# The end of a two-layer decoder kernel: a gate moved into the weights, a shorter final norm, stores on two queues

## The chip, the cores and the metric

The kernel runs on one core of a Trainium2 chip. A core has engines that run side by side, each with its own list of instructions: TensorE (matmul), VectorE (elementwise work), ScalarE (activation functions, copies and casts), GpSimd and SyncE, whose queue issues most of the transfers. An engine waits at an instruction until what it needs has been signalled by the others. The metric is the device time of one execution in microseconds; lower is better.

## The reference, cut to what matters

The reference is a decoder trunk of two layers over 512 rows of 1024 columns in fp32. Only its end counts here: the MLP of the second layer, its gated residual, and the final norm over the columns of each row.

```python
for layer in range(DEPTH):
    ...
    shift, scale, gate = ada_modulation(c, ada_w[layer, 1], ada_b[layer, 1])
    h = rms_norm(x, norm_w[layer, 1]) * (1.0 + scale) + shift
    x = x + (gate * squared_relu_mlp(h, mlp_w1[layer], mlp_w2[layer])).astype(x.dtype)
return rms_norm(x, final_norm_w)

def rms_norm(x, w):
    y = xf * lax.rsqrt(jnp.mean(xf * xf, axis=-1, keepdims=True) + EPS)
    return (y * w.astype(jnp.float32)).astype(x.dtype)
```

`gate` has one value for each of the 1024 columns, so gate * (g @ w2) is the same as g @ (w2 with its columns scaled by the gate).

## The kernel before, in words

Each fp32 operand of a matmul is split into a high part (`wh`, `gh`; a cast by ScalarE) and a low part (`wl`, `gl`; raw minus high, by VectorE), and each product takes three matmuls: high by high, low by high, high by low. The second layer's down projection runs over eight groups of 512 inner features. Six of them are done as pairs in a scheme that combines quarter products. The last two groups (`gs[0]` and `gs[1]`, r = 0 and 1) go through `Pair.direct`, the last stage of the kernel.

In `direct` the output is cut into two column halves (q = 0, 1; 512 columns each) and four row blocks of 128 rows (`hf`, `i`; tb = 2 hf + i). For each q and each row block, 24 matmuls of 128x512 fill one bank: r = 0, 1, then f = 0 to 3, then the three of each product. The banks are named sc, sc, tp, po in turn, again for q = 1. The weights are split ahead by `split`, four tiles of 128x512 each: keys 11 and 21 for q = 0 (made earlier), key 12 (r = 0) and key 22 (r = 1) for q = 1. Key 12 is split at the start of `direct`, key 22 within the fourth q = 0 block, after its matmuls are written and before its evacuation.

The other work: `gate_b[q]` is the gate spread over all rows (by TensorE, then copied from the bank by ScalarE); `fwb[q]` is the final norm's weight, loaded into all rows; `xT` is the residual, loaded from a scratch tensor. In the trace and in the order lists all of these are tiles called `end`: in the lists end_8978 and end_8979 are `gate_b[0]` and `gate_b[1]`, end_8980 and end_8981 are `fwb[0]` and `fwb[1]`, end_8970 to end_8977 are `xT`. The partial sums of the earlier pairs are the tiles x_132 to x_137 and two `acc`; at the start of `direct` 16 VectorE operations multiply each by the gate and add the residual. The raw weights are w_1413 to w_1416 (key 12) and w_1417 to w_1420 (key 22).

After a block VectorE multiplies the bank by the gate and adds it to the sum tile; ScalarE squares the sum with a row total into a column of `ss` (`square`). With q = 1 `finish` makes the row factor: small VectorE and ScalarE operations on one column, among them a logarithm and an exponential for the inverse square root, and one refining step. Then VectorE scales both halves by the row factor and by `fwb`, and SyncE's queue stores each.

The order: from this stage on VectorE and TensorE keep the order in which the program is written (`V` and `TE` are `_InOrder`; every one of their instructions shows as line 81, that of the helper). The lists of ScalarE and of the queue are set by the scheduler.

Of the kernel before, what the change touches and what calls it, by code (L numbers as in the profile page):

```python
# [15 lines left out]
ALU = mybir.AluOpType  # L16
AX = mybir.AxisListType

P = 128
T = 512  # L20
D = 1024
# [5 lines left out]
EPS = 1e-6  # L27
# [57 lines left out]
def trunk(ctx: ExitStack, tc: tile.TileContext, ins, out):  # L85
    nc = tc.nc
    V, S, G, TE = nc.vector, nc.scalar, nc.gpsimd, nc.tensor
# [6 lines left out]
    wsplit = ctx.enter_context(tc.tile_pool(name="wsplit", bufs=4))  # L94
# [9 lines left out]
    def nm(s):  # L104
        uid[0] += 1
        return f"{s}_{uid[0]}"
# [4 lines left out]
    def sc_ps():  # L111
        return ps_sc.tile([P, 512], F32, tag="sc", name=nm("sc"))
# [27 lines left out]
    rows = fpool.tile([P, 2 * P], F32, name="rows")  # L140
# [44 lines left out]
    def square(j, hf, n_, fast=False):  # L185


        xj, sums = x[j][:, HALVES[hf]], sqsum.get(hf)
        if n_ == 0:
            sums = sqsum[hf] = [wk("sqsum", (P, HALF))]  # L190
        elif n_ == 1 and fast:
            sums.append(pp.tile([P, HALF], F32, tag="sqsum2", name=nm("sqsum2")))
        i = n_ % len(sums)
        if n_ == 0 or n_ == 1 and fast:
            S.activation(sums[i], xj, AF.Square)
            return lambda: None
        sq = wk("acc", (P, T))[:, 0:HALF] if fast else wk("sq", (P, HALF))
        S.activation(sq, xj, AF.Square)

        def add():  # L200
            e = V if i == 1 or n_ == ND - 1 else G
            e.tensor_tensor(sums[i], sums[i], sq, op=ALU.add)
            if n_ == ND - 1 and fast:
                V.tensor_tensor(sums[0], sums[0], sums[1], op=ALU.add)

        return add
# [125 lines left out]
    def load(dst, src):  # L332

        if isinstance(V, _InOrder):
            anchor[0] = Q.dma_start(dst, src)
        else:
            with tc.issue_after(anchor[0].ins):
                nc.sync.dma_start(dst, src)
# [183 lines left out]
    class Seam(Steps):  # L522
# [18 lines left out]
        def square(self, kind, hf, j):  # L541
            n_ = self.counts[kind, hf] = self.counts.get((kind, hf), -1) + 1
            self.adds[hf, j] = square(j, hf, n_, kind == "y")
# [51 lines left out]
    def bank4():  # L595
        four[0] += 1
        return (sc_ps, sc_ps, tp_ps, po_ps)[(four[0] - 1) % 4]()
# [7 lines left out]
    V, S, G, TE = [_InOrder(tc, e) for e in (V, S, G, TE)]  # L605
# [740 lines left out]
    V, S, G, TE = nc.vector, nc.scalar, nc.gpsimd, nc.tensor  # L1346
# [187 lines left out]
    V, S, G, TE = [_InOrder(tc, e) for e in (V, S, G, TE)]  # L1534
# [13 lines left out]
    V, S, G, TE = nc.vector, nc.scalar, nc.gpsimd, nc.tensor  # L1548
# [6 lines left out]
    wsplit2 = spare.pop()  # L1555
    fp = ctx.enter_context(tc.tile_pool(name="fin", bufs=1))
    ss = fp.tile([P, 16], F32, name="ss")
# [3 lines left out]
    for tb in range(NT):  # L1561
        rt = wraw.tile([P, RAW], F32, tag="raw", name=nm("xT"))
        for q in range(2):
            ps = sc_ps()
# [8 lines left out]
    sums = {(k, i): free[2 * k - 2 + i] for k in range(1, 8) for i in range(2)}  # L1573
    C11, C12, C21, C22 = 2, 3, 4, 5

    def each(*all_):

        all_ = [a[0] if isinstance(a, list) and len(a) == 1 else a for a in all_]
        if not any(isinstance(a, list) for a in all_):
            return [all_]  # L1580
        return [[a[i] if isinstance(a, list) else a[:, i * HALF : (i + 1) * HALF] for a in all_] for i in range(2)]
# [3 lines left out]
    class Pair:  # L1585
# [9 lines left out]
                        load(t, mlp1.w2[:, 4 * (2 * n + r) + f, q * T : (q + 1) * T])  # L1595
                        self.raw[f"{r + 1}{q + 1}", f] = t

        def split(self, key, pool=wsplit):

            w = []  # L1600
            for f in range(4):
                if f % 2 == 0:
                    th = pool.tile([P, RAW], F32R, tag="wh", name=nm("wh"))
                    tl = pool.tile([P, RAW], F32R, tag="wl", name=nm("wl"))
                cs = slice(f % 2 * T, (f % 2 + 1) * T)
                S.copy(th[:, cs], self.raw[key, f])  # L1606
                V.tensor_tensor(tl[:, cs], self.raw[key, f], th[:, cs].bitcast(F32), op=ALU.subtract)  # L1607
                w.append((th[:, cs], tl[:, cs]))
            return w
# [87 lines left out]


        def direct(self, weights):
            later = [self.split("12", wsplit2)]  # L1700
            for q in range(2):
                for tb in range(NT):
                    for t, g_, x_ in each(sums[2 + tb // 2 * 2 + q, tb % 2], gate_b[q], xT[tb, q]):
                        V.tensor_tensor(t, t, g_, op=ALU.mult)
                        V.tensor_tensor(t, t, x_, op=ALU.add)
            for q in range(2):
                w = later if q else weights
                for hf in range(2):
                    for i in range(2):
                        k = 2 + 2 * hf + q  # L1710
                        ps = bank4()
                        ts = slice((2 * hf + i) * P, (2 * hf + i + 1) * P)
                        for r in range(2):
                            gh, gl = self.gs[r]
                            for f in range(4):
                                wh, wl = w[r][f]
                                TE.matmul(ps, gh[:, f, ts], wh, start=r + f == 0, stop=False)
                                TE.matmul(ps, gh[:, f, ts], wl, start=False, stop=False)
                                TE.matmul(ps, gl[:, f, ts], wh, start=False, stop=r == 1 and f == 3)
                        if k == 4 and i == 1:  # L1720
                            later.append(self.split("22"))
                        (t,) = sums[k, i]
                        V.tensor_tensor(ps, ps, gate_b[q], op=ALU.mult)
                        V.tensor_tensor(t, t, ps, op=ALU.add)
                        self.square(k, hf, q, i)
                        if q:
                            self.finish(k - 1, k, hf, i)

        def square(self, k, hf, q, i):
            (t,) = sums[k, i]  # L1730
            tb = 2 * hf + i
            S.activation(junk, t, AF.Square, accum_out=ss[:, 2 * tb + q : 2 * tb + q + 1])

        def finish(self, k0, k1, hf, i):
            tb = 2 * hf + i
            r, y = ss[:, 8 + tb : 9 + tb], ss[:, 12 + tb : 13 + tb]
            V.tensor_tensor(r, ss[:, 2 * tb : 2 * tb + 1], ss[:, 2 * tb + 1 : 2 * tb + 2], op=ALU.add)
            V.tensor_scalar(r, r, 1.0 / D, EPS, op0=ALU.mult, op1=ALU.add)
            S.activation(y, r, AF.Ln)
            S.activation(y, y, AF.Exp, scale=-0.5)  # L1740
            V.scalar_tensor_tensor(r, r, y, y, op0=ALU.mult, op1=ALU.mult)
            V.tensor_scalar(r, r, -0.5, 1.5, op0=ALU.mult, op1=ALU.add)
            V.tensor_tensor(r, r, y, op=ALU.mult)
            for q, k in enumerate((k0, k1)):
                (t,) = sums[k, i]
                V.scalar_tensor_tensor(t, t, r, fwb[q], op0=ALU.mult, op1=ALU.mult)
                nc.sync.dma_start(out[0, tb * P : (tb + 1) * P, q * T : (q + 1) * T], t)

    def merge():

# [35 lines left out]
    V, weights = _InOrder(tc, nc.vector), []  # L1786
# [8 lines left out]
    gate_b, fwb = [late_tile(8 + q) for q in range(2)], [late_tile(10 + q) for q in range(2)]  # L1795
    junk = late_tile(12)
    for q in range(2):
        load(fwb[q], ins["final_norm_w"][q * T : (q + 1) * T].partition_broadcast(P))
        ps = (tp_ps, po_ps)[q]()
        for j in range(4):  # L1800
            TE.matmul(ps[:, j * P : (j + 1) * P],
                      mlp1.gate[:, 4 * q + j : 4 * q + j + 1].broadcast_to([P, P]), ident, start=True, stop=True)
        S.copy(gate_b[q], ps)
        for tb in range(NT):
            load(xT[tb, q], xT_dram[tb][:, q * T : (q + 1) * T])
# [24 lines left out]
```

## Time and profile before

| | |
|---|---|
| time, median of 3 runs | 1001.47 us (998.39 to 1001.85) |
| profiled execution, own time | 997.38 us |
| its span, first to last instruction | 995.7 us |
| granted TensorE clock, mean | 0.995 |
| TensorE busy | 968.0 us, 97% |
| VectorE busy | 675.7 us, 68% |
| ScalarE busy | 490.2 us, 49% |
| GpSimd busy | 188.0 us, 19% |

The shares are means over the whole span; the stage of the change is its last 50 us. Whether an operation there counts is read from who waits for whom: an engine that waits for nothing but TensorE has time to spare, and TensorE's next block is late only if its weights or its bank are late.

### The profile page before, as it was taken

Reading aid. Unit: us, or ns where it says so; the run is one execution under the profiler, and the core shown is the slowest. Engines: PE = TensorE matmul, PEld = TensorE weight load, DVE = VectorE, ACT = ScalarE, POOL = GpSimd, SP = SyncE. Lnnn points to the kernel's source line nnn. Section 1 sums busy time; section 2 is a strip of 40 time slices with the busy share of each in tenths; the row PEclk is TensorE's granted clock in tenths of the full one; section 3 lists DMA queues with packets and bytes.
Section 4 is the critical chain, followed back from the end, with each engine's and each line's share of the span. In section 5 each row is a group of like instructions: output and inputs, shape, how many; then the busy total and the mean of one; then the engine's idle time right before and its main releaser. Section 6 shows DMA issues by size and latency. Waiting matters only on the chain.

```text
span 995.7 us, 14343 instructions
## 1 busy us (share of the span) xinstructions
PE 968.0 (97%) x5392; PEld 804.6 (81%) x5392; DVE 675.7 (68%) x1181; ACT 490.2 (49%) x913; POOL 188.0 (19%) x136
## 2 busy tenths in 40 slices
PE   6989999998999999999999999999999999999996
PEld 5568888788987778787777899998788788778885
DVE  3678886666886757666665427859557856886385
ACT  6566657665542433333343435665664544455511
POOL 0033436456120201111122345400000000000000
PEclk9999999999999999999999999999999999999999
DMA  9973566442375656465566312172451253042202
GB/s 309 339 173 106 170 188 217 154 141 64 107 240 183 221 157 214 134 208 187 170 211 207 107 49 83 60 245 78 127 169 43 85 161 93 0 152 102 74 34 84
DMA packets 119367, 145.57 MB, mean 146 GB/s; under 512 B 5782, under 2 KB 86018, under 8 KB 119298
## 3 DMA queue, kind: packets, MB, share of 16 engines
q1 hardware_dynamic: 119138, 144.59, 46.9%
q8 instruction: 42, 0.69, 0.3%
q14 instruction: 27, 0.22, 0.1%
q10 hardware_dynamic: 160, 0.07, 0.0%
HBM read 140.25 MB, written 4.39 MB: 145 GB/s over the span
## 4 chain that ended last, share of the span: by engine, by line
PE 87%; DVE 5%; issue 2%; DMA 2%; POOL 2%; ACT 1%; SPq 1%; DVEq 0%; POOLq 0%; ACTq 0%
PE mm L81 33%; PE mm L370 10%; PE sc L81 10%; PE mm L372 10%; PE mm L371 10%; PE po L81 5%; PE tp L81 5%; PE ad L81 2%; DMA adaw<-in_ada_w 1%; SPq L81 1%; DVE wl L1607 1%; POOL wl L81 1%; PE ad L283 1%; POOL sqsum L81 1%; DMA xin<-in_x 1%
## 5 line engine op out<-in xcount | busy, mean ns | idle before, releaser
L364 ACT CAST wh<-w 128x1024 fp32r<-128x1024 f32 x82 | 85.8, 1050 | 110.0 <-PE mm L371 80.2
L81 PE MATMUL mm<-hh,wl 128*128 128x512 f32 (+1 forms) x312 | 116.1, 379 | 2.0 <-DVE wl L366 2.0
L366 DVE TENSOR_TENSOR wl<-w,wh 128x1024 fp32r<-128x1024 f32 x76 | 100.0, 1320 | 24.3 <-ACT wh L364 23.2
L81 PE MATMUL mm<-hh,wh 128*128 128x512 f32 (+1 forms) x312 | 116.3, 380 | 0.0
L81 PE MATMUL mm<-hl,wh 128*128 128x512 f32 (+1 forms) x312 | 115.5, 377 | 0.0
L81 POOL TENSOR_TENSOR wl<-w,wh 128x1024 fp32r<-128x1024 f32 x36 | 87.6, 2444 | 79.9 <-ACT wh L81 77.1
L371 PE MATMUL mm<-hl,wh 128*128 128x512 f32 (+1 forms) x256 | 95.7, 376 | 0.0
L372 PE MATMUL mm<-hh,wl 128*128 128x512 f32 (+1 forms) x256 | 95.5, 375 | 0.0
L370 PE MATMUL mm<-hh,wh 128*128 128x512 f32 (+1 forms) x256 | 94.3, 377 | 0.0
L1606 ACT CAST wh<-w 128x512 fp32r<-128x512 f32 x100 | 56.9, 619 | 53.2 <-PE po L81 21.9
L370 PE MATMUL mm<-gh,wh 128*128 128x512 f32 x192 | 75.9, 395 | 0.0
L371 PE MATMUL mm<-gl,wh 128*128 128x512 f32 x192 | 74.8, 390 | 0.0
L372 PE MATMUL mm<-gh,wl 128*128 128x512 f32 x192 | 74.8, 390 | 0.0
L81 PEld LDWEIGHTS mm<-hh,wl 128*128 128x128 f32 x312 | 58.7, 188 | 15.6 <-DVE wl L366 4.0
L81 PEld LDWEIGHTS mm<-hh,wh 128*128 128x128 f32 x312 | 58.9, 189 | 11.6 <-ACT wh L364 0.6
L81 PEld LDWEIGHTS mm<-hl,wh 128*128 128x128 f32 x312 | 58.9, 189 | 11.3
L1607 DVE TENSOR_TENSOR wl<-w,wh 128x512 fp32r<-128x512 f32 x84 | 54.7, 689 | 17.7 <-ACT wh L1606 17.5
L248 DVE SCALAR_TENSOR_TENSOR acc<-adaw,sc,acc 128x512 f32<-128x512 f32 x60 | 46.7, 778 | 21.0 <-DMA adaw<-in_ada_w 20.4
L274 POOL TENSOR_TENSOR adaw<-adaw 128x512 f32<-128x512 f32 x12 | 15.7, 1306 | 232.4 <-ACT adaw L272 199.4
L375 DVE SCALAR_TENSOR_TENSOR x<-mm,mod,x 128x512 f32<-128x512 f32 x48 | 35.7, 746 | 31.8 <-PE mm L372 31.8
L81 ACT CAST wh<-w 128x1024 fp32r<-128x1024 f32 (+1 forms) x44 | 43.8, 1004 | 25.8 <-DMA w<-in_attn_w_in 9.3
L372 PEld LDWEIGHTS mm<-hh,wl 128*128 128x128 f32 x256 | 48.2, 188 | 9.6 <-issue 0.8
(499 smaller groups left out, 2488.9 us busy)
## 6 DMA issues: line engine op xcount, KB each, us to landing
w<-in_mlp_w SPq DMA_DIRECT2D x98, 512.0 KB, 4.1
adaw<-in_ada_w SPq DMA_DIRECT2D x92, 512.0 KB, 4.6
w<-in_mlp_w SPq DMA_DIRECT2D x64, 256.0 KB, 3.7
w<-in_attn_w_in SPq DMA_DIRECT2D x8, 512.0 KB, 3.6
w<-in_attn_w_out SPq DMA_DIRECT2D x8, 512.0 KB, 3.5
w<-in_attn_w_in SPq DMA_DIRECT2D x8, 392.0 KB, 7.9
xin<-in_x SPq DMA_DIRECT2D x4, 512.0 KB, 5.7
adaw<-in_ada_w SPq DMA_DIRECT2D x8, 256.0 KB, 6.1
```

Source lines behind the costliest of these rows:

```text
L81: return lambda *args, **kw: self.tc.keep_in_program_order(f(*args, **kw))
L248: V.scalar_tensor_tensor(acc, rv, sk, acc, op0=ALU.mult, op1=ALU.add)
L274: G.tensor_tensor(rv[:, 0], rv[:, 0], rv[:, 1], op=ALU.add)
L283: TE.matmul(ps[32 * j : 32 * j + 32], one_col[:, 31 - r : 63 - r], self.acc[:, j * P : (j + 1) * P], start=True, stop=True)
L364: S.copy(th[:, :n], rt[:, :n])
L366: return w, lambda e: e.tensor_tensor(tl[:, :n], rt[:, :n], th[:, :n].bitcast(F32), op=ALU.subtract)
L370: TE.matmul(ps, wh, ah, start=start, stop=False)
L371: TE.matmul(ps, wh, al, start=False, stop=False)
L372: TE.matmul(ps, wl, ah, start=False, stop=stop)
L375: V.scalar_tensor_tensor(x[j][:, ts], ps, g, x[j][:, ts], op0=ALU.mult, op1=ALU.add)
L1606: S.copy(th[:, cs], self.raw[key, f])
L1607: V.tensor_tensor(tl[:, cs], self.raw[key, f], th[:, cs].bitcast(F32), op=ALU.subtract)
```

## The change

- `split` takes a `scale`: for keys 12 and 22 each raw weight tile is multiplied by `gate_b[1]` in place, by VectorE, before its cast. The gate multiply of the bank stays for q = 0 only.
- With q = 0 `square` now also scales the row total (divide by 1024, add EPS) and multiplies the sum tile by `fwb[0]`.
- `finish` has one small operation ahead of the logarithm instead of two and two behind the exponential instead of three; the factor -0.5 of the refining step goes into `fwb`, which is scaled by it after its load.
- The first column half is multiplied by the row factor on ScalarE and stored from ScalarE's queue; the second stays on VectorE and SyncE's queue.

```diff
-        def split(self, key, pool=wsplit):
+        def split(self, key, pool=wsplit, scale=None):
 
             w = []
             for f in range(4):
+                if scale is not None:
+                    V.tensor_tensor(self.raw[key, f], self.raw[key, f], scale, op=ALU.mult)
                 if f % 2 == 0:
                     th = pool.tile([P, RAW], F32R, tag="wh", name=nm("wh"))
...
         def direct(self, weights):
-            later = [self.split("12", wsplit2)]
+            later = [self.split("12", wsplit2, gate_b[1])]
...
                         if k == 4 and i == 1:
-                            later.append(self.split("22"))
+                            later.append(self.split("22", scale=gate_b[1]))
                         (t,) = sums[k, i]
-                        V.tensor_tensor(ps, ps, gate_b[q], op=ALU.mult)
+                        if q == 0:
+                            V.tensor_tensor(ps, ps, gate_b[q], op=ALU.mult)
                         V.tensor_tensor(t, t, ps, op=ALU.add)
                         self.square(k, hf, q, i)
...
             S.activation(junk, t, AF.Square, accum_out=ss[:, 2 * tb + q : 2 * tb + q + 1])
+            if q == 0:
+                r = ss[:, 8 + tb : 9 + tb]
+                V.tensor_scalar(r, ss[:, 2 * tb : 2 * tb + 1], 1.0 / D, EPS, op0=ALU.mult, op1=ALU.add)
+                V.tensor_tensor(t, t, fwb[q], op=ALU.mult)
 
         def finish(self, k0, k1, hf, i):
             tb = 2 * hf + i
             r, y = ss[:, 8 + tb : 9 + tb], ss[:, 12 + tb : 13 + tb]
-            V.tensor_tensor(r, ss[:, 2 * tb : 2 * tb + 1], ss[:, 2 * tb + 1 : 2 * tb + 2], op=ALU.add)
-            V.tensor_scalar(r, r, 1.0 / D, EPS, op0=ALU.mult, op1=ALU.add)
+            V.scalar_tensor_tensor(r, ss[:, 2 * tb + 1 : 2 * tb + 2], 1.0 / D, r, op0=ALU.mult, op1=ALU.add)
             S.activation(y, r, AF.Ln)
             S.activation(y, y, AF.Exp, scale=-0.5)
             V.scalar_tensor_tensor(r, r, y, y, op0=ALU.mult, op1=ALU.mult)
-            V.tensor_scalar(r, r, -0.5, 1.5, op0=ALU.mult, op1=ALU.add)
-            V.tensor_tensor(r, r, y, op=ALU.mult)
-            for q, k in enumerate((k0, k1)):
-                (t,) = sums[k, i]
-                V.scalar_tensor_tensor(t, t, r, fwb[q], op0=ALU.mult, op1=ALU.mult)
-                nc.sync.dma_start(out[0, tb * P : (tb + 1) * P, q * T : (q + 1) * T], t)
+            V.scalar_tensor_tensor(r, r, 3.0, y, op0=ALU.subtract, op1=ALU.mult)
+            rows = out[0, tb * P : (tb + 1) * P, :]
+            (t0,), (t1,) = sums[k0, i], sums[k1, i]
+            S.mul(t0, t0, r)
+            V.scalar_tensor_tensor(t1, t1, r, fwb[1], op0=ALU.mult, op1=ALU.mult)
+            nc.scalar.dma_start(rows[:, 0:T], t0)
+            nc.sync.dma_start(rows[:, T:D], t1)
...
         load(fwb[q], ins["final_norm_w"][q * T : (q + 1) * T].partition_broadcast(P))
+        V.tensor_scalar(fwb[q], fwb[q], -0.5, None, op0=ALU.mult)
```

TensorE's list is the same row for row, and GpSimd's too. The lists of VectorE and ScalarE differ only from the last up-projection block on.

VectorE at the start of `direct`, before: the last `gl`, the split of key 12, the partial sums.

```order
L81 TENSOR_TENSOR gl_8769<-r_8965,gh_8768 128x512
L81 TENSOR_TENSOR wl_9006<-w_1413_8786,wh_9005 128x512
L81 TENSOR_TENSOR wl_9006<-w_1414_8788,wh_9005 128x512
L81 TENSOR_TENSOR wl_9012<-w_1415_8790,wh_9011 128x512
L81 TENSOR_TENSOR wl_9012<-w_1416_8792,wh_9011 128x512
L81 TENSOR_TENSOR x_132<-x_132,end_8978 128x512
```

The same place after the change.

```order
L81 TENSOR_TENSOR gl_8769<-r_8965,gh_8768 128x512
L81 TENSOR_SCALAR end_8980<-end_8980 128x512
L81 TENSOR_SCALAR end_8981<-end_8981 128x512
L81 TENSOR_TENSOR w_1413_8786<-w_1413_8786,end_8979 128x512
L81 TENSOR_TENSOR wl_9009<-w_1413_8786,wh_9008 128x512
L81 TENSOR_TENSOR w_1414_8788<-w_1414_8788,end_8979 128x512
L81 TENSOR_TENSOR wl_9009<-w_1414_8788,wh_9008 128x512
```

The two scalings of `fwb` now stand ahead of the split, and a gate multiply stands ahead of each subtraction; w_1415 and w_1416 follow in the same way.

VectorE at the end of the q = 0 blocks, before: the third evacuation (bank tp), the split of key 22, the fourth evacuation (bank po).

```order
L81 TENSOR_TENSOR tp_9089<-tp_9089,end_8978 128x512
L81 TENSOR_TENSOR x_136<-x_136,tp_9089 128x512
L81 TENSOR_TENSOR wl_9143<-w_1417_8794,wh_9142 128x512
L81 TENSOR_TENSOR wl_9143<-w_1418_8796,wh_9142 128x512
L81 TENSOR_TENSOR wl_9149<-w_1419_8798,wh_9148 128x512
L81 TENSOR_TENSOR wl_9149<-w_1420_8800,wh_9148 128x512
L81 TENSOR_TENSOR po_9117<-po_9117,end_8978 128x512
```

The same place after the change.

```order
L81 TENSOR_TENSOR tp_9099<-tp_9099,end_8978 128x512
L81 TENSOR_TENSOR x_136<-x_136,tp_9099 128x512
L81 TENSOR_SCALAR ss<-ss 128x1
L81 TENSOR_TENSOR x_136<-x_136,end_8980 128x512
L81 TENSOR_TENSOR w_1417_8794<-w_1417_8794,end_8979 128x512
L81 TENSOR_TENSOR wl_9156<-w_1417_8794,wh_9155 128x512
L81 TENSOR_TENSOR w_1418_8796<-w_1418_8796,end_8979 128x512
L81 TENSOR_TENSOR wl_9156<-w_1418_8796,wh_9155 128x512
```

A small operation on `ss`, which reads ScalarE's row total, and the multiply by `fwb[0]` now stand behind each q = 0 evacuation, so also ahead of the split; the split has a multiply ahead of each subtraction, and w_1419 and w_1420 follow in the same way.

VectorE's last rows, the fourth q = 1 block, before.

```order
L81 TENSOR_TENSOR po_9274<-po_9274,end_8979 128x512
L81 TENSOR_TENSOR acc_6834<-acc_6834,po_9274 128x512
L81 TENSOR_TENSOR ss<-ss 128x1
L81 TENSOR_SCALAR ss<-ss 128x1
L81 SCALAR_TENSOR_TENSOR ss<-ss 128x1
L81 TENSOR_SCALAR ss<-ss 128x1
L81 TENSOR_TENSOR ss<-ss 128x1
L81 SCALAR_TENSOR_TENSOR x_137<-x_137,ss,end_8980 128x512
L81 SCALAR_TENSOR_TENSOR acc_6834<-acc_6834,ss,end_8981 128x512
```

ScalarE's last rows after the change; VectorE keeps for this block the add, three small operations and the scaling of acc_6834.

```order
L1735 ACTIVATE end_8982,ss<-acc_6834 128x512
L1745 ACTIVATE ss<-ss 128x1
L1746 ACTIVATE ss<-ss 128x1
L1751 ACTIVATE x_137<-x_137,ss 128x512
L1753 DMA out<-x_137 128x512
```

The scaling of x_137 and its store have moved from VectorE and SyncE's queue to ScalarE and its queue.

## Rows read from the trace of the kernel before

**Rows 1.** Page, part 4: shares of the chain that ended last.

```profile
PE 87%; DVE 5%; issue 2%; DMA 2%; POOL 2%; ACT 1%; SPq 1%; DVEq 0%; POOLq 0%; ACTq 0%
```

**Rows 2.** Chain in order of time from 944 us: start, length, what.

```profile
943.83 10.93 PE sc L81 x48
...
965.64 10.88 PE sc L81 x48
...
987.44 0.71 DVE po L81
```

**Rows 3.** Timeline of VectorE, 938 to 970: start, length, operation, [idle before, releaser].

```profile
945.53 0.69 DVE L81 TENSOR_TENSOR gl<-r,gh 128x512 fp32r<-128x512 f32 x1 [6.40 <-ACT r L417]
946.14 2.49 DVE L81 TENSOR_TENSOR wl<-w,wh 128x512 fp32r<-128x512 f32 x4
948.54 8.06 DVE L81 TENSOR_TENSOR x<-x,end 128x512 f32<-128x512 f32 x12
...
959.18 0.69 DVE L81 TENSOR_TENSOR sc<-sc,end 128x512 f32<-128x512 f32 x1
...
963.17 2.49 DVE L81 TENSOR_TENSOR wl<-w,wh 128x512 fp32r<-128x512 f32 x4
```

**Rows 4.** Timeline of SyncE's queue and of ScalarE near 942.

```profile
941.75 0.42 SPq L81 DMA_DIRECT2D end<-in_final_norm_w  x1
...
941.85 1.14 ACT L1606 CAST wh<-w 128x512 fp32r<-128x512 f32 x2 [1.66 <-PE mm L81]
```

**Rows 5.** DMA issues from 941.5 to 942.1: size, us from issue to landing.

```profile
end<-in_final_norm_w SPq DMA_DIRECT2D x1, 256.0 KB, 5.1
```

**Rows 6.** Timeline from the last add to the last store's issue.

```profile
988.17 0.69 DVE L81 TENSOR_TENSOR acc<-acc,po 128x512 f32<-128x512 f32 x1
988.89 0.63 ACT L1732 ACTIVATE end<-acc 128x512 f32<-128x512 f32 x1 [3.86 <-DVE acc L81]
...
989.65 0.16 DVE L81 TENSOR_TENSOR ss<-ss 128x1 f32<-128x1 f32 x1 [0.79 <-ACT end L1732]
...
990.03 0.20 ACT L1739 ACTIVATE ss<-ss 128x1 f32<-128x1 f32 x1 [0.41 <-DVE ss L81]
...
990.50 0.22 DVE L81 SCALAR_TENSOR_TENSOR ss<-ss 128x1 f32<-128x1 f32 x1 [0.51 <-ACT ss L1740]
...
991.14 0.75 DVE L81 SCALAR_TENSOR_TENSOR x<-x,ss,end 128x512 f32<-128x512 f32 x1
...
991.92 0.33 SPq L1747 DMA_DIRECT2D out<-x  x1
992.58 0.33 SPq L1747 DMA_DIRECT2D out<-acc  x1
```

**Rows 7.** Groups by line and form: count, busy us, mean ns, idle before.

```profile
L1606 ACT CAST wh<-w 128x512 fp32r<-128x512 f32 x100 | 56.9, 619 | 53.2 <-PE po L81 21.9 <-PE mm L81 21.1 <-PE sc L81 9.7
...
L272 ACT ACTIVATE adaw<-adaw,sc 128x512 f32<-128x512 f32 x24 | 16.1, 716 | 41.0 <-DMA adaw<-in_ada_w 37.9 <-DVE wl L366 3.1
...
L81 DVE TENSOR_TENSOR x<-x,end 128x512 f32<-128x512 f32 x12 | 7.8, 689 | 0.2
...
L81 DVE TENSOR_SCALAR acc<-adaw,sc 128x512 f32<-128x512 f32 x11 | 5.3, 484 | 7.2 <-DMA adaw<-in_ada_w 6.0 <-PE ad L81 1.2
```

**Rows 8.** Windows: PE, PEld, DVE, ACT, POOL busy, then PEclk, DMA share, GB/s.

```profile
70.00:72.00 2.00, 1.73 (x6) 1.42 (x7) 1.81 (x3) 1.94 (x5) 0.00 (x0) 0.59 1.08 364
72.00:74.00 2.00, 2.00 (x6) 1.51 (x5) 1.93 (x5) 1.98 (x4) 0.50 (x1) 0.56 0.50 182
...
992.00:994.00 2.00, 0.00 (x0) 0.00 (x0) 0.56 (x1) 0.00 (x0) 0.00 (x0) 0.50 0.62 236
```

**Rows 9.** Timeline of TensorE, 69 to 74 us.

```profile
69.25 0.33 PE L81 MATMUL sc<-kh,q 128*128 128x128 f32 x1 [2.33 <-DVE q L81]
...
70.66 1.19 PE L81 MATMUL po<-glr,wgh 128*128 128x512 f32 x2 [0.27 <-DVE q L81]
...
73.78 0.39 PE L81 MATMUL mm<-hl,wh 128*128 128x512 f32 x1
```

## The prediction, made before the changed kernel ran

> **What bounds the kernel now.** I read the chain of waits first, then its last 50 us, then VectorE and ScalarE over the same stretch. The chain is TensorE for 87% of the span [rows 1]. In the last stage (`Pair.direct`) it is TensorE without a gap from 943.83 to 987.4 us: eight blocks of 24 matmuls, 5.44 us each (10.88 / 2), four of column half q=0, then four of q=1 [rows 2]. Only after the last block do the other engines carry the end: from 987.44 to the last store's issue at 992.58 [rows 2, 6]. So an edit here pays only if it shortens those 5.14 us, and costs only if it makes one of the eight blocks wait. Blocks of q=1 need the weights of keys 12 and 22, both made by VectorE and ScalarE while q=0 runs.
>
> The question is therefore when the split of 22 is ready. In the kernel before, VectorE starts its four `wl` subtractions at 963.17 and has done them by 965.66 [rows 3]. Block q=1, 0 begins at 965.64 [rows 2] and reaches 22 in its second half; the last `wl` (f=3) is read by matmul 23 of 24, after 22 x 0.227 us (5.44 / 24), at 970.6. The slack is **5.0 us**.
>
> VectorE works strictly in the order of its list: the four `wl` of key 12 had their casts by 942.99 (the later pair of casts is the one at 941.85) [rows 4], yet started at 946.14, behind a `gl` that waited 6.40 us for ScalarE [rows 3]. So each wait that the change puts into VectorE's list holds all that follows.
>
> **The change part by part.** Until 943 us the lists are the same. What is new on VectorE up to the last `wl` of 22:
>
> 1. The two `fwb` scalings stand right behind the last `gl`. `fwb[1]` is issued at 941.75 [rows 4] and lands 5.1 us later [rows 5], at 946.85. ScalarE loses its casts of key 12 ahead of that `gl`, so the `gl` comes earlier, but VectorE then waits for the load. A 128x512 TENSOR_SCALAR takes 0.48 us [rows 7]; with a hand-over of 0.03 on either side (988.17 + 0.69 to 988.89 [rows 6]) the first gate multiply starts at 947.39, where the first `wl` stood at 946.14: **+1.25**.
>
> 2. Split of 12: four subtractions in a row took 2.40 us (946.14 to 948.54), 0.60 from one start to the next [rows 3]. Now for each f the order is multiply, cast on ScalarE, subtract, and the next multiply stands behind that subtract. One turn: multiply 0.69, hand-over 0.03, cast 0.62, hand-over 0.03, subtract 0.60 to the next start. The 0.69 and 0.62 are the means of their groups [rows 7]. 1.97 x 4 = 7.88 us: **+5.48**.
>
> 3. The 16 operations on the partial sums keep their 10.64 us (948.54 to 959.18) [rows 3].
>
> 4. The three q=0 evacuations that stand ahead of the split of 22 took 3.99 us (959.18 to 963.17) [rows 3]. Each now also holds a small operation that waits for ScalarE's square, and behind it a 128x512 multiply by `fwb[0]`. One turn: 0.73 for the gate multiply (987.44 to 988.17) [rows 2, 6], 1.48 from the add to the small operation (988.17 to 989.65), 0.16 + 0.03 for it [rows 6], 0.60 for the multiply. 3.00 x 3 = 9.00 us: **+5.01**. What is queued behind this wait is the split of 22, and TensorE waits for that.
>
> 5. Split of 22: three turns of 1.97 and a last one to the end of its subtract, 2.06, are 7.97 us against 2.49 [rows 3]: **+5.48**.
>
> Sum: 1.25 + 5.48 + 5.01 + 5.48 = 17.2 us, so the last `wl` comes at about 982.9. Less the slack of 5.0, block q=1, 0 ends **12.2 us** later, at about 983.3 instead of 971.08 (965.64 + 5.44). On the way TensorE waits 1.7 us for the bank (block q=0, 0 is evacuated at about 967.4), works 2.7 us on key 12, then idles 6.2 us until the first cast of 22 at about 976.3. Blocks 1 to 3 follow in 16.3 us as before; VectorE finishes the fourth q=0 evacuation some 3 us after the split and has caught up by the third q=1 block, since a q=1 turn on it (0.7 us and the small chain, 4.2 us in all) is shorter than 5.44 us.
>
> 6. The end gets shorter. The gate multiply on the bank goes: 0.73. From the last add to the last issue it was 4.41 us (988.17 to 992.58) [rows 6]. Now: 1.48 to the first small operation; 0.25 for it (0.22 + 0.03, the three-operand form); 0.47 for the two activations (990.03 to 990.50); 2 x 0.25; then 0.75 for the row scaling on VectorE and 0.02 to the issue: 3.47 [rows 6]. On ScalarE the other half is an activation with a column as scale, 0.72 us [rows 7], beside it. So 0.94 + 0.73 = 1.67 us sooner. Both stores then start at once instead of 0.66 us apart (991.92, 992.58) [rows 6]. The trace shows no such pair; in the 2 us window of the end the DMA engines were busy 0.62 of the time [rows 8]. The loss lies between nothing and the 0.66 us of head start; I take 0.3, about the idle share of that head start. Net **-1.37**.
>
> The Trainium skill, "DMA: Bandwidth & Descriptors", section "Issuing engines are not separate DMA queues", says that transfers issued from two engines share the same DMA engines and save only issue time. By it the second queue is worth the issue of one store, 0.33 us; counting the two as independent would make this term -1.67. No run here has shown it yet.
>
> The other removals (gate multiplies and small operations of the first three q=1 blocks, two stores in a row on one queue) lie under TensorE's blocks and give nothing.
>
> **Net**: +12.2 - 1.37 = +10.8 us. Against the profiled execution's own 997.38 us (span 995.7 and 1.7 around it) that is 1008.2. The three timed runs have their median 4.1 us above the profiled one, at 1001.47; carried over: **1012.3 us**, 1.1% slower. I count 0.5% (5 us) as about what a measurement of this kernel can tell from no change.
>
> **The rivals.**
>
> A. *The waits on VectorE cost nothing, only its new work does.* Then 1.25 + 4 x 0.60 + 3 x 0.79 + 4 x 0.60 = 8.4 us; less 5.0 of slack and 1.37 at the end it is +2.0, 1003.5 us, no change. For it: ScalarE has time to run ahead. Against it: each multiply feeds its own cast, and the order puts the next multiply behind the subtract that waits for that cast.
>
> B. *Not slower: the split of 22 stays under the q=0 blocks.* This needs the last `wl` by 970.6, so at most 5.0 us of delay on VectorE; up to that point TensorE never waits, and only the end counts: 1001.47 - 1.37 = 1000.1 us. For it: in the old list VectorE has 5.0 us in hand. Against it: the new work alone, without any wait, is 8.4 us.
>
> C. *TensorE's clock falls in the gap.* After a wait of 2.33 us on VectorE and some small matmuls [rows 9], the granted clock read 0.59 and 0.56 in the two windows from 70 to 74 us [rows 8], a mix of 2.4 and 1.2 GHz, and the seven 512-column matmuls from 70.66 to 73.78 [rows 9] followed each other at 0.446 us, against 0.227 at full clock. The gap here is longer, 6.2 us, so the clock should fall. While TensorE gets three matmuls per 1.97 us turn, even 0.446 us each (1.34 us) is hidden. It costs only if the clock is still low when block q=1, 1 begins; the early stretch paid 7 x 0.219 = 1.5 us. Here 7 us lie between the first cast and the dense blocks, longer than that whole episode, so I take 0 in the sum and keep +1.5: 1013.8 us.
>
> The Trainium skill, "TensorE: Matmul & The Clock Gate", section "HAM oscillation — how this bites in real kernels", says that waits between bursts of matmuls throttle the clock so that the next burst starts slow. By that rule rival C comes true in full.
>
> **How the numbers follow.** Forecast 0.78, C 0.12 (both slower), A 0.06 and B 0.04 (both within 0.5%; the drift of a run may make 0.02 of B read faster). The added time in forecast and C is at least 8.9 us (no wait for `fwb[1]`, 1.25; the tail gain whole, 0.3; 0.05 us less in each of the eight turns, 0.4) and at most 13.7 (the clock, 1.5; hand-overs of 0.09 in the sixteen crossings of the splits, 1.0; the whole head start lost, 0.36). The base is the timed runs, 998.39 to 1001.85: 1007.3 to 1015.6. Widened a little below for a part of A: **1006.5 to 1016**. Faster 0.02, same 0.09, slower 0.89.
>
> **What would show it.** Right: TensorE waits some 6 us once and about 1 us several times, on ScalarE `wh` and VectorE `wl`, between 967 and 984; VectorE's rows alternate multiply and subtract about 1 us apart in both splits; the last block ends near 999.6; the last store issues 3.5 us after the last add. Wrong: TensorE runs the eight blocks without a gap (B), or the gaps add up to less than 5 us (A), or matmuls of q=1 blocks 1 to 3 are 0.43 us apart (C). A `fwb[1]` load that lands before 945.5 would take 1.25 us off; an error in the 1.97 us turn counts eightfold.

## The result

The changed kernel took 1012.05 us (median of 6 runs, 1010.19 to 1015.19), the kernel before 1001.29 us beside it (6 runs, 998.39 to 1001.97). The ratio is **1.0124, 95% interval 1.0102 to 1.0145**: slower by 10.2 to 14.5 us. The forecast was 1012.3 us in 1006.5 to 1016, slower with a chance of 0.89.

The two profiled executions stand further apart, 1012.92 against 997.38 us, and 3.41 us of that lies ahead of the change: the first matmul of `direct` starts at 943.59 us before and at 947.00 after, though the program is the same until just ahead of it. Over all the profiles of this study that start lies between 943.59 and 948.51 with no link to what was edited that these runs show, and the kernel before alone ranged from 996.88 to 1004.07 us in the 25 runs beside e1 to e4, so it is taken as drift between executions. From here on times are counted from that first matmul; a time "in the times of before" is one shifted by the difference of the two starts. The stage has two parts: the **blocks**, up to the end of the last matmul, and the **tail**, from there to the end of the span.

| kernel | blocks, us | tail, us | together |
|---|---|---|---|
| before | 43.81 | 8.30 | 52.11 |
| after | 57.03 | 7.17 | 64.20 |
| difference | +13.22 | -1.13 | +12.09 |
| predicted | +12.2 | -1.37 | +10.8 |

### The profile page after: what moved, and what is told of

Same layout as the page of the kernel before. It is cut to its first block, busy times and chain, and to the rows that moved or that the text cites. A ratio compares the mean times of both kernels' runs of the same rounds, so it can differ in the third digit from the quotient of the medians.

```text
span 1011.2 us, 14353 instructions
## 1 busy us (share of the span) xinstructions
PE 976.2 (97%) x5392; PEld 807.8 (80%) x5392; DVE 679.2 (67%) x1183; ACT 494.0 (49%) x917; POOL 186.1 (18%) x136
## 4 chain that ended last, share of the span: by engine, by line
PE 82%; DVE 8%; issue 3%; DMA 3%; ACT 2%; POOL 1%; SPq 1%; POOLq 0%; ACTq 0%; DVEq 0%
PE mm L81 32%; PE mm L370 10%; PE mm L372 10%; PE mm L371 10%; PE sc L81 9%; PE po L81 4%; PE tp L81 4%; DMA adaw<-in_ada_w 2%; PE ad L81 1%; DVE x L81 1%; DVE acc L81 1%; SPq L81 1%; DVE wl L1609 1%; POOL wl L81 1%; PE ad L283 1%
```

## The profile after

The page's chain gives TensorE less and VectorE more than in [rows 1]:

```profile
PE 82%; DVE 8%; issue 3%; DMA 3%; ACT 2%; POOL 1%; SPq 1%; POOLq 0%; ACTq 0%; DVEq 0%
```

The waits of TensorE from 944 to 1006 us (what it waited for: us in total, times, longest). Before, this answer was empty.

```profile
PE sc L81 <- ACT wh L1608: 5.6, 1, 5.6
PE sc L81 <- DVE x L81: 0.7, 1, 0.7
```

VectorE's timeline (start, length, operation, [idle before, releaser]), which answers to [rows 3]:

```profile
947.79 0.69 DVE L81 TENSOR_TENSOR gl<-r,gh 128x512 fp32r<-128x512 f32 x1 [5.25 <-ACT r L417]
948.40 0.42 DVE L81 TENSOR_SCALAR end<-end 128x512 f32<-128x512 f32 x1
949.28 0.43 DVE L81 TENSOR_SCALAR end<-end 128x512 f32<-128x512 f32 x1 [0.47 <-DMA end<-in_final_norm_w]
949.62 0.68 DVE L81 TENSOR_TENSOR w<-w,end 128x512 f32<-128x512 f32 x1
951.00 0.69 DVE L81 TENSOR_TENSOR wl<-w,wh 128x512 fp32r<-128x512 f32 x1 [0.69 <-ACT wh L1608]
951.61 0.68 DVE L81 TENSOR_TENSOR w<-w,end 128x512 f32<-128x512 f32 x1
...
957.55 8.05 DVE L81 TENSOR_TENSOR x<-x,end 128x512 f32<-128x512 f32 x12
...
968.18 0.69 DVE L81 TENSOR_TENSOR sc<-sc,end 128x512 f32<-128x512 f32 x1
...
970.38 0.15 DVE L81 TENSOR_SCALAR ss<-ss 128x1 f32<-128x1 f32 x1 [0.79 <-ACT end L1735]
...
976.92 0.69 DVE L81 TENSOR_TENSOR w<-w,end 128x512 f32<-128x512 f32 x1
978.34 0.69 DVE L81 TENSOR_TENSOR wl<-w,wh 128x512 fp32r<-128x512 f32 x1 [0.74 <-ACT wh L1608]
...
984.34 0.69 DVE L81 TENSOR_TENSOR wl<-w,wh 128x512 fp32r<-128x512 f32 x1 [0.69 <-ACT wh L1608]
```

Both splits show what was forecast: multiply, wait for the cast, subtract. A turn is 1.99 us (949.62 to 951.61; forecast 1.97), the split of 12 takes 7.93 us (949.62 to 957.55), and the wait for ScalarE, 0.69 to 0.74 us, returns in every turn. The three evacuations take 8.74 us (968.18 to 976.92), each with its wait for the square. The last `wl` is done at 985.03, which is 981.62 in the times of before.

When it was needed is read best from TensorE's timeline of the kernel before, the first matmul of block q = 1, 0 and the one that reads the last `wl`:

```profile
965.48 0.39 PE L81 MATMUL sc<-wh,gh 128*128 128x512 f32 x1
...
970.47 0.39 PE L81 MATMUL sc<-wl,gh 128*128 128x512 f32 x1
```

After the change that matmul starts at 985.08, 981.67 in the times of before: 11.2 us late. TensorE's timeline over the gap and behind it:

```profile
978.36 0.79 PE L81 MATMUL sc<-wh,gh 128*128 128x512 f32 x1 [5.62 <-ACT wh L1608]
...
984.36 0.79 PE L81 MATMUL sc<-wh,gh 128*128 128x512 f32 x1
985.08 0.79 PE L81 MATMUL sc<-wl,gh 128*128 128x512 f32 x1
985.67 0.63 PE L81 MATMUL sc<-wh,gl 128*128 128x512 f32 x1
986.10 0.63 PE L81 MATMUL sc<-wh,gh 128*128 128x512 f32 x1
986.53 0.63 PE L81 MATMUL sc<-wl,gh 128*128 128x512 f32 x1
...
989.34 0.39 PE L81 MATMUL sc<-wh,gl 128*128 128x512 f32 x1
...
992.99 0.39 PE L81 MATMUL tp<-wh,gh 128*128 128x512 f32 x1
```

And its windows (length, busy time of PE, PEld, DVE, ACT, POOL, then the granted clock, DMA share, GB/s), which answer to [rows 8]:

```profile
972.00:974.00 2.00, 0.74 (x4) 0.28 (x2) 1.15 (x4) 0.72 (x2) 0.00 (x0) 1.00 0.00 0
974.00:976.00 2.00, 0.00 (x0) 0.00 (x0) 1.36 (x3) 0.51 (x1) 0.00 (x0) 0.86 0.00 0
...
986.00:988.00 2.00, 2.00 (x6) 1.51 (x6) 1.15 (x4) 0.72 (x2) 0.00 (x0) 0.50 0.00 0
988.00:990.00 2.00, 2.00 (x8) 1.56 (x7) 0.71 (x2) 1.09 (x4) 0.00 (x0) 0.72 0.00 0
990.00:992.00 2.00, 2.00 (x10) 1.64 (x9) 1.13 (x3) 0.76 (x2) 0.00 (x0) 1.00 0.00 0
```

The clock falls to 0.50 (1.2 GHz) in the gap, stays there through the turns with three matmuls each, and is still there when the dense block begins at 986.10: its matmuls follow each other at 0.43 us, as the early ones of [rows 9] did, until 1.00 is back. That block takes 6.89 us to the next one's first matmul at 992.99, 1.45 more than 5.44. Another 0.57 is lost in the last turn: behind the `wl` at 985.03 two more matmuls of 0.227 us would have let the block begin at 985.53. The clock so costs 2.0 us, and with the 11.2 us this is the whole 13.2 of the blocks.

The tail, from the last add to the stores, which answers to [rows 6]:

```profile
1004.07 0.69 DVE L81 TENSOR_TENSOR acc<-acc,po 128x512 f32<-128x512 f32 x1 [2.10 <-PE po L81]
...
1006.66 0.75 DVE L81 SCALAR_TENSOR_TENSOR acc<-acc,ss,end 128x512 f32<-128x512 f32 x1
1007.41 0.37 ACTq L1753 DMA_DIRECT2D out<-x  x1
1007.44 0.33 SPq L1754 DMA_DIRECT2D out<-acc  x1
```

From the last add to the first of the two issues it is 3.34 us (before 4.41 to the last issue), and the gate multiply of 0.73 ahead of it is gone: 1.80 us sooner. But from issue to the end of the span it is now 3.8 us (1007.41 to 1011.2), where it was 3.1 from the last issue (992.58 to 995.7), so the 0.66 us of head start are lost in whole. The DMA share in 40 equal slices shows why. First the kernel before, 991.5 to 995.7 us:

```profile
DMA  0000000000019999999999899200000000000000
```

Then the kernel after, 1007 to 1011.2 us, in slices of the same length:

```profile
DMA  0000000000009999999999999300000000000000
```

Both show one block of 14 or 15 slices of 0.105 us, nearly all at full load: the bytes of two stores, 0.52 MB in about 1.5 us, without a hole. Before, the second store joined while the first one's bytes still moved, so the head start of 0.66 us had already been used in full; starting both at once gives nothing beyond the earlier issue.

## The experiments

The theory was that of the prediction: VectorE's list decides, the last `wl` of key 22 comes late by the sum of the delays less one slack of 5.0 us. The rivals are that the tail's new form or VectorE's extra passes slow the kernel in another way, and that the clock is the real loss. Each ratio is against the kernel before on the same chip. The runs e2 to e6 undo or move one part; e7 and e9 came when e1 had missed its number.

| kernel | ratio to before, interval | blocks | tail | together |
|---|---|---|---|---|
| e1, gate kept on the banks | 1.0025, 1.0010 to 1.0040 | 47.86 | 7.88 | 55.74 |
| e2, before with the fold alone | 1.0078, 1.0050 to 1.0106 | 51.13 | 7.54 | 58.67 |
| e3, multiplies ahead of subtractions | 1.0069, 1.0045 to 1.0093 | 52.13 | 7.21 | 59.34 |
| e4, new work on GpSimd | 1.0044, 1.0027 to 1.0060 | 49.08 | 7.03 | 56.11 |
| e5, spare matmuls in the gap | 1.0109, 1.0069 to 1.0148 | 56.81 | 7.15 | 63.96 |
| e6, both stores on one queue | (one run, 1013.31 us) | 56.93 | 7.12 | 64.05 |
| e7, e3 and small work moved back | 1.0001, 0.9985 to 1.0016 | 43.82 | 7.17 | 50.99 |
| e9, e1 and small work moved back | 1.0007, 0.9992 to 1.0021 | 43.82 | 7.92 | 51.74 |

### e1: the fold undone

```diff
-            later = [self.split("12", wsplit2, gate_b[1])]
+            later = [self.split("12", wsplit2)]
...
-                            later.append(self.split("22", scale=gate_b[1]))
+                            later.append(self.split("22"))
...
-                        if q == 0:
-                            V.tensor_tensor(ps, ps, gate_b[q], op=ALU.mult)
+                        V.tensor_tensor(ps, ps, gate_b[q], op=ALU.mult)
```

> The changed kernel with one part undone: the gate of the second column half multiplies the bank again, as before, and is not put into the weights; the rest of the change stays (norm factors, first-half weight multiply, ScalarE scaling, two queues). The stage is counted from the first matmul of direct to the end of the span: 52.1 us before, 64.2 after the change. Theory (the two splits cost about 5.5 us each through multiply-cast-subtract turns, and VectorE had 5.0 us in hand): without them the last low part of key 22 comes at 16 operations, three longer evacuations (2.9 us each) and a split of 2.5 us, which uses up the 5.0 us of slack and hardly more, so TensorE waits 0 to 1 us; the end is 0.73 us longer than in the changed kernel. Stage 51.7 to 52.7 us, time within 0.1% of before. Rival (the new multiply and small operation behind each first-half evacuation, or the two queues, are what costs): stage stays near 62 us.

Most of the loss goes with the fold, but not all, and the expectation was missed by some 3.5 us. TensorE's wait, then two rows of ScalarE's timeline and one of VectorE's, and three windows:

```profile
PE sc L81 <- DVE wl L81: 2.1, 1, 2.1
```

```profile
962.38 1.14 ACT L1608 CAST wh<-w 128x512 fp32r<-128x512 f32 x2 [16.11 <-PE po L81]
963.42 0.63 ACT L1734 ACTIVATE end<-x 128x512 f32<-128x512 f32 x1
```

```profile
964.18 0.15 DVE L81 TENSOR_SCALAR ss<-ss 128x1 f32<-128x1 f32 x1 [2.09 <-ACT end L1734]
```

```profile
970.00:972.00 2.00, 0.55 (x2) 0.49 (x3) 1.96 (x5) 0.01 (x1) 0.00 (x0) 1.00 0.00 0
972.00:974.00 2.00, 2.00 (x8) 1.59 (x7) 1.97 (x4) 0.00 (x0) 0.00 (x0) 0.74 0.00 0
974.00:976.00 2.00, 2.00 (x6) 1.52 (x6) 1.15 (x3) 0.72 (x2) 0.00 (x0) 0.50 0.00 0
```

Here ScalarE's list has two casts of key 22 ahead of the first square, so VectorE's small operation waits 2.09 us instead of 0.79. With it the work of the first column half ahead of key 22 eats more than the slack: TensorE waits 2.1 us for the first `wl` of key 22, whose matmul comes 2.25 us later than before, and then the clock falls, so that the blocks lose 4.05 us, 1.8 of it to the clock. The longer wait for the square, 1.30 us, is ScalarE's order; without it, as an estimate from these rows, TensorE would have waited about 1 us, which the expectation allowed. e9 takes away the operation that waits for the square.

### e2: the fold alone, on the kernel before

The edit takes the fold into the kernel before: `split` with its `scale`, and the lines that e1 undoes.

> The kernel before with one part of the change alone: the gate of the second column half put into the weights of keys 12 and 22, and its bank multiply dropped; norm, scaling and stores as before. Theory: the splits take 7.9 and 8.1 us instead of 2.4 and 2.5, the first starts 1.1 us earlier since ScalarE reaches the last up-projection activation sooner, so the last low part of 22 comes at about 975.7 on the time scale of before, 5.1 us past the need at 970.6; the end is 0.73 us shorter. Stage 52.1 + 5.1 - 0.7 = 56.5 us if TensorE's clock stays up (it is not idle for long, but gets only three matmuls per 2 us turn), up to 58.5 if it falls. Rival (cost only from work, not from waits): stage 52 us.

TensorE's waits from 943 to 1006 us:

```profile
PE sc L81 <- ACT wh L1608: 1.7, 3, 0.7
PE sc L81 <- DVE wl L81: 0.5, 2, 0.2
```

There is no long gap, only turns with three matmuls, and the clock still falls: 0.99 in 972 to 974, 0.50 in the three windows from 974 to 980. The last `wl` is done at 976.62 (975.7 in the times of before) and its matmul comes 5.3 us late; the blocks lose 7.32, and the 2.0 beyond that are the clock again. The stage, 58.67 us, is 0.2 above the upper end of what was expected. The prediction's two terms of +5.48 less its slack make 5.96; the split here starts 1.15 us earlier than in the kernel before, and the mechanism holds by itself. The tail is 0.76 shorter: the gate multiply.

### e3: multiplies ahead of the subtractions

```diff
             for f in range(4):
-                if scale is not None:
+            if scale is not None:
+                for f in range(4):
                     V.tensor_tensor(self.raw[key, f], self.raw[key, f], scale, op=ALU.mult)
+            for f in range(4):
```

> The changed kernel with the same instructions in another order: in each scaled split the four gate multiplies stand first, then the four subtractions, so ScalarE's casts run beside VectorE. Theory (the waits for the casts cost, not the multiplies): a split takes 4.8 us instead of 7.9 and 8.1, the last low part of 22 comes 6.4 us earlier than in the changed kernel, TensorE's gap shrinks from 11 to about 4.7 us plus what its clock takes. Stage 64.2 - 6.4 = 57.8 us with the clock's 2.1 us still in it, 55.7 if the clock stays up. Rival (only the amount of work counts): stage stays at 64 us.

The splits take 4.8 and 4.9 us instead of 7.93 and 8.11, with the same operations: the difference, 3.1 and 3.2 us, is the wait for the cast in each turn. The blocks lose 8.32 instead of 13.22 us, so the stage is 59.34 and not the 57.8 of the expectation: a gain less by about 1.4 than those 6.3 us. Of this 0.7 is a later `fwb[1]` (VectorE waited 1.15 us for it, against 0.47). The grouped multiplies also delay the first `wl`, and it is now the one that TensorE waits for: its matmul comes 5.8 us late, where the last `wl` alone would have made it 5.6. The other 2.5 of the 8.32 are the clock's, against 2.0. It goes half the way to rival A of the prediction: the splits no longer wait, the evacuations still do.

### e4: the new work on GpSimd

```diff
-            later = [self.split("12", wsplit2, gate_b[1])]
+            for key in ("12", "22"):
+                for f in range(4):
+                    G.tensor_tensor(self.raw[key, f], self.raw[key, f], gate_b[1], op=ALU.mult)
+            for q in range(2):
+                G.tensor_scalar(fwb[q], fwb[q], -0.5, None, op0=ALU.mult)
...
+            later = [self.split("12", wsplit2)]
...
-                            later.append(self.split("22", scale=gate_b[1]))
+                            later.append(self.split("22"))
...
-                V.tensor_tensor(t, t, fwb[q], op=ALU.mult)
+                G.tensor_tensor(t, t, fwb[q], op=ALU.mult)
```

> The changed kernel with its added work taken off VectorE's path to key 22: the eight weight tiles are multiplied by the gate on GpSimd, which is idle there, as are the scalings of the norm weight and the multiply of the first half by it; the split of key 12 stands behind the 16 operations on partial sums; the four small operations on the first half's row totals stand behind the last first-half evacuation. Theory: GpSimd needs 8 x 1.3 = 10.4 us from about 947, done by 958, the casts of 22 can't start before 961.6 anyway; TensorE runs the eight blocks without a wait; only the shorter end counts, 7.1 instead of 8.3 us. Stage 51.0 us, 1.1 us under before, time 0.1% under it. Rival (GpSimd and VectorE slow each other, so that VectorE's 0.69 us operations stretch): stage 52 us or more.

The expectation of 51.0 failed, the rival came true. Groups from 945 to 977 us (count, busy us, mean ns, idle before):

```profile
L81 DVE TENSOR_TENSOR x<-x,end 128x512 f32<-128x512 f32 x12 | 14.5, 1240 | 0.2
L1704 POOL TENSOR_TENSOR w<-w,end 128x512 f32<-128x512 f32 x8 | 13.5, 1717 | 0.0
```

While GpSimd multiplies, VectorE's operation takes 1240 ns instead of the 689 of [rows 7]. Its 16 sum operations last 19.3 us (946.59 to 965.91), 8.7 more than before. The work had left VectorE's list, and its time had not. TensorE's waits from 943 to 1006 us:

```profile
PE sc L81 <- DVE x L81: 2.6, 1, 2.6
PE sc L81 <- DVE wl L81: 1.7, 2, 1.0
```

The first is for the bank of block q = 1, 0, which VectorE had evacuated late. Through these waits the granted clock read 1.00 in every 2 us window from 960 to 996 us: here the blocks' 5.27 us are waits alone.

### e5: spare matmuls in the gap

```diff
                         for r in range(2):
+                            if q and k == 3 and i == 0 and r:
+                                busy = mm_ps()
+                                for _ in range(24):
+                                    TE.matmul(busy, self.gs[0][0][:, 0, ts], w[0][0][0], start=True, stop=True)
```

> The changed kernel with 24 extra matmuls of 128x512 into a spare bank, which nobody reads, between the two halves of block q=1, 0, where TensorE idles 5.6 us. Theory (the gap lets TensorE's clock fall to 1.2 GHz, and that costs 2.1 us: 0.6 in the last turn of key 22 and 1.6 in the seven slow matmuls behind it): with TensorE busy through the gap the granted clock stays at 1.00 and the stage falls from 64.2 to about 62.1 us. Rival (the slow matmuls have another cause, such as their operands): no change, 64.2 us. If the sparse turns alone lower the clock, it falls later and part of the 2.1 us stays.

TensorE's timeline, then its windows:

```profile
969.88 5.60 PE L81 MATMUL mm<-wh,gh 128*128 128x512 f32 x24
975.68 0.51 PE L81 MATMUL sc<-wh,gh 128*128 128x512 f32 x1 [0.20 <-ACT wh L1608]
```

```profile
976.00:978.00 2.00, 1.26 (x4) 0.48 (x3) 1.32 (x3) 0.62 (x1) 0.00 (x0) 1.00 0.00 0
978.00:980.00 2.00, 1.45 (x4) 0.58 (x3) 1.26 (x3) 0.62 (x1) 0.00 (x0) 0.67 0.00 0
980.00:982.00 2.00, 1.97 (x4) 0.79 (x3) 1.31 (x3) 0.62 (x1) 0.00 (x0) 0.50 0.00 0
```

The products of the spare matmuls are used nowhere. They keep the clock at 1.00 over the gap, and it falls behind them, in the turns. So the blocks gain 0.2 us and no more, where up to 2.1 were expected. Filling the turns too was not tried; that the clock costs 2.0 us in the changed kernel rests on the spacing of its matmuls, not on a run in which the clock stayed up.

### e6: both stores on SyncE's queue

```diff
-            nc.scalar.dma_start(rows[:, 0:T], t0)
+            nc.sync.dma_start(rows[:, 0:T], t0)
```

> The changed kernel with both stores of a row block issued by SyncE's queue again. After the last add the changed kernel needs 3.35 us to the two issues and 3.78 us from there to the end of the span. Theory (both transfers share the same DMA engines, so the second queue saves at most the issue): the end comes 0 to 0.35 us later, 7.1 to 7.5 us after the last add starts. Rival (the second queue gives real overlap): 0.7 us later or more. Rival (two queues at once disturb each other): earlier than in the changed kernel.

The two issues on the queue:

```profile
1007.85 0.33 SPq L1753 DMA_DIRECT2D out<-x  x1
1008.27 0.38 SPq L1754 DMA_DIRECT2D out<-acc  x1
```

They come 0.42 us apart, and the tail is 7.12 us against 7.17: the second queue is worth nothing that this one profile can show. The rule that the prediction cited, of the Trainium skill, "DMA: Bandwidth & Descriptors", section "Issuing engines are not separate DMA queues", agrees with this; it would have granted the 0.33 us of one issue, and not even that appears.

### e7 and e9: the first half's small work behind the split

In e7 on top of e3, in e9 on top of e1: the `fwb` scalings, the four small operations and the four multiplies by `fwb[0]` stand behind the fourth q = 0 evacuation. The part of the edit that both share:

```diff
             for q in range(2):
                 w = later if q else weights
+                if q:
+                    self.first_half()
...
-            if q == 0:
-                r = ss[:, 8 + tb : 9 + tb]
-                V.tensor_scalar(r, ss[:, 2 * tb : 2 * tb + 1], 1.0 / D, EPS, op0=ALU.mult, op1=ALU.add)
-                V.tensor_tensor(t, t, fwb[q], op=ALU.mult)
...
+        def first_half(self):
+            for q in range(2):
+                V.tensor_scalar(fwb[q], fwb[q], -0.5, None, op0=ALU.mult)
+            for tb in range(NT):
+                (t,) = sums[2 + tb // 2 * 2, tb % 2]
+                r = ss[:, 8 + tb : 9 + tb]
+                V.tensor_scalar(r, ss[:, 2 * tb : 2 * tb + 1], 1.0 / D, EPS, op0=ALU.mult, op1=ALU.add)
+                V.tensor_tensor(t, t, fwb[0], op=ALU.mult)
...
-        V.tensor_scalar(fwb[q], fwb[q], -0.5, None, op0=ALU.mult)
```

> The changed kernel with two edits: the four gate multiplies of a key are issued ahead of its four subtractions (as in e3), and the two scalings of fwb, the four small norm steps on ss and the four multiplies of t0 by fwb[0] stand behind the fourth evacuation of the first column half, so behind the split of key 22. Nothing is left out. Theory (VectorE's path to the last wl of key 22 sets the loss): counted in the times of before, multiplies from 944.9, split of 12 in 4.8 (measured in e3) to 949.7, sixteen sum operations 10.6 to 960.3, three evacuations at 1.33 to 964.3, split of 22 in 4.8 to 969.1, against a need of 970.6: TensorE never waits, the clock stays at 1.00, the blocks take the 43.8 us of before, the tail 7.2 of after, stage 51.0 against 52.1 of before; about 1 us faster, ratio 0.999. Rival (the tail's operations and the second store queue themselves cost it, or TensorE is slowed by VectorE's extra passes): the wait for key 22 is gone and the stage is still 54 or more.

> The changed kernel without the fold (the gate of the second half is again multiplied into the sums, as in e1), and the fwb scalings, small norm steps and multiplies of t0 moved behind the split of key 22 as in e7. Nothing is left out. Theory: the 3.5 us that e1 lost over its expectation came from the small operations of the first half ahead of the split of 22 (which also stood behind squares on ScalarE); moved away, VectorE is as early as before, no wait, blocks 43.8, tail 7.9 as in e1, stage 51.7 against 52.1 of before: no measurable difference, ratio 0.9995. Rival (e1's loss came from ScalarE's order, casts of 22 ahead of the square, or from the clock): the wait of about 2 us on wl of key 22 stays and the stage is about 55.

Both came out as worked out, 50.99 for 51.0 and 51.74 for 51.7. VectorE in e7, the whole split of key 22:

```profile
969.36 2.49 DVE L81 TENSOR_TENSOR w<-w,end 128x512 f32<-128x512 f32 x4
971.77 2.49 DVE L81 TENSOR_TENSOR wl<-w,wh 128x512 fp32r<-128x512 f32 x4
```

The first matmul of `direct` is at 948.51 in this execution, so the last `wl`, at 974.26, is 969.3 in the times of before, 1.1 ahead of its matmul at 970.47 (the first `wl` has 0.9 in hand). TensorE waits nowhere, the granted clock is 1.00 throughout, and the blocks take 43.82 us, as before. In e9 ScalarE's list still has two casts of key 22 ahead of the first square, as in e1:

```profile
964.28 1.14 ACT L1608 CAST wh<-w 128x512 fp32r<-128x512 f32 x2 [16.11 <-PE po L81]
965.33 0.63 ACT L1736 ACTIVATE end<-x 128x512 f32<-128x512 f32 x1
```

TensorE doesn't wait either. So the new form of the tail costs the blocks nothing, and e1's rest needs the small work ahead of the split: ScalarE's order alone costs nothing, and could add its 1.30 us in e1 only because an operation of VectorE waited for the square. The fold costs nothing once its multiplies are grouped and nothing else new stands ahead of key 22. The blocks' 13.2 us are the place of these operations in VectorE's list, and the clock behind it.

The tail's gain of 1.1 us is then left alone: together 50.99 against 52.11. In the timed runs it can't be told from nothing (ratio 1.0001, 0.9985 to 1.0016). No kernel tried here beats the one before by more than a measurement tells.

## Why the prediction was right

The sign, the mechanism and the place were those of the forecast, and the time as well, by luck to within 0.3 us: the stage took 1.3 us more than forecast (+12.09 against +10.8), less than what executions of one kernel differ by. By its steps:

| step | predicted | measured |
|---|---|---|
| 1, `fwb` scalings and their load | +1.25 | +0.1 (first gate multiply at 949.62, 946.21 in the times of before; 946.14 there) |
| 2, split of 12 | 7.88 us | 7.93 us |
| 3, sum operations | 10.64 us | 10.63 us |
| 4, three evacuations | 9.00 us | 8.74 us |
| 5, split of 22 | 7.97 us | 8.11 us (976.92 to 985.03) |
| TensorE late by the weights | 12.2 us | 11.2 us |
| C, the clock | 0 in the sum, up to +1.5 | +2.0 us |
| 6, tail | -1.37 us | -1.13 us |

Three terms were mis-sized, and the first two offset each other in part. The slack was also read a little too large: 5.0 from the chain row at 965.64 [rows 2], 4.8 from the timeline, where the block starts at 965.48.

**Step 1** took the load's 5.1 us from [rows 5]. In the changed kernel it landed after 4.0, and the wait was 0.47 us. One duration of one transfer was taken as fixed; in e3, with the same load, the wait was 1.15 us. Why it varies was not followed up.

**The clock** was the step of the argument that failed. The prediction saw that it would fall, and let the low stretch end within the turns because the early episode was short [rows 8, 9]. But the turns are themselves sparse: the clock read 0.50 all through them and rose only in the dense block behind, as e2 and e5 show too. Rival C was thus true in its cost, beside the forecast and not in place of it: its sign, matmuls of block q = 1, 1 that are 0.43 us apart, came for the first seven. The rule cited, of the Trainium skill, "TensorE: Matmul & The Clock Gate", section "HAM oscillation — how this bites in real kernels", has the burst behind a wait start slow, and the trace agrees with it: the dense block began at 0.50. The waits of about 1 us that were forecast for the turns did not come, as at half the clock three matmuls fill nearly the whole turn.

**Step 6** took 0.3 us for the lost head start, from a share of 0.62 in a window of 2 us [rows 8], and it was 0.66, the whole. The window held idle time ahead of and behind the transfer; the finer slices shown above, which the trace of before already had, would have told it.

The rivals: A fell since each turn did wait (e3 has the same work without the waits, and its blocks are 4.9 us shorter). B fell, and e7 meets its condition, `wl` by 970.6, with the result that B worked out: no wait, the tail's gain alone.

## What to carry to other kernels

Ask of each operation that is added to an engine in strict order what is queued behind it and when that is needed: the added work cost the blocks 13 us as it stood ahead of the last weights, and nothing with the multiplies grouped and the rest moved behind them. Slack is spent once: without the clock's share the fold alone made TensorE 5.3 us late (e2) and the rest alone 2.3 (e1), but together 11.2, since each of the two had used the same 5 us. And a step that hands a tile to another engine and back should be issued for all tiles before the first answer is awaited.

## What the runs showed of the hardware

- GpSimd and VectorE slow each other: a 128x512 VectorE operation on two tiles went from 0.69 to 1.24 us while GpSimd multiplied, and GpSimd's own took 1.72 us. The Trainium skill, "SBUF — State Buffer", section "Who interferes with whom", says that a VectorE instruction with two inputs there contends with a GpSimd instruction that reads it; the trace agrees.
- The granted clock fell after a wait of 2.1 us (e1), and without a long wait when TensorE got three matmuls per 2.0 us turn (e2). It stayed at 1.00 in e4 through waits of 2.6, 1.0 and 0.7 us, so the length of a wait alone does not tell whether it falls; what does is left open here. Where it fell, the loss behind it was 1.8 to 2.5 us, in e1 nearly as large as the wait itself.
- Two 256 KB stores moved in about 1.5 us whether they were issued together or 0.66 us apart, on one queue or two.
